# The samples' attention with the cache as the moving operand, and six held splits at the end of a down chain

## The chip, the core and the metric

The kernel runs on one core of a Trainium2 chip. Its engines work side by side, each through its own queue in order: TensorE (PE; its weight loads are PEld) multiplies, VectorE (DVE) and ScalarE (ACT) work elementwise, GpSimd (POOL) does the rest of the elementwise work, and SyncE (SP) issues most of the transfers. Matmul results land in PSUM, of which there are eight banks; the other data is in SBUF, with 128 partitions. The metric is device time in microseconds of one launch.

## The reference

One layer of a decoder trunk is computed for a prompt of 1024 tokens and for 8 samples of one token each. All of it is float32. What bears on the change, cut down:

```python
# attention over a window of 128 keys with sinks; 16 query heads, 4 key heads, head size 64
s = jnp.einsum('...qhgd,...khd->...hgqk', qg, kb) * (SWA_HD ** -0.5)
p = jax.nn.softmax(jnp.concatenate([s, sink], axis=-1), axis=-1)[..., :-1]
return jnp.einsum('...hgqk,...khd->...qhgd', p, vb)
...
# a sample: the cache's last 127 rows and its own new row
kc = jnp.concatenate([st['k'], kk], axis=1)
vc = jnp.concatenate([st['v'], vv], axis=1)
...
x = x + gt2 * ((jax.nn.silu(gc) * up) @ lp['w_ffn_down'])     # 2816 -> 1024
```

Before the attention stand a normalisation and one input projection; beside it runs a gated delta rule with a short convolution; after it an output projection and a feed-forward block with a convolution. The last line is the down projection.

## The kernel before

**Precision.** A large product splits both operands into a high and a low part and adds three matmuls (`mm3`, lines 180 to 182). A split is two instructions: ACT writes the high part (line 129), and VectorE or POOL the rest (line 130). Small products, such as the samples', are plain float32 matmuls. The profile has two matmul records for one of these.

**Order.** The instructions are not queued as the program text has them. A planner simulates the kernel when it is built, and at each moment takes for an engine the ready instruction that is earliest by priority. Priority follows the text, except that `later` and `weave` move pieces back by a number of places, and that `issue_after` forbids instructions to stand ahead of a given one on the same engine. On the chip each queue then runs in the planned order, whatever is ready.

**Attention.** `attention` goes over four groups of query heads, one for each key head, and each group over eight blocks of 128 tokens (`attention_block`). A block's way is: scores on PE (lines 614 and 615), a masked copy (lines 618 and 620), maximum and sink (`m` and `es`, lines 622 to 627), exponentials with their sums (line 630), the inverse denominator `den` (lines 631 and 632), scaling (lines 635 and 637), transposes into `pt` and masks (lines 642 and 646), the value product into `pv` (line 652) and a copy out (line 654). Pieces of other work, such as input projections and convolution tiles (lines 778 to 790), fill the gaps.

**Samples.** `sample_cache` runs before the fourth group. It loads the keys and values of 8 samples into tiles of four samples (`halves`), and lays the queries into `qa`, one block of eight columns for each sample and each pair of key heads; the rest of `qa` is zeroed at line 684 and the copies are at line 688. In the first half of the fourth group, `sample_keys` transposes the keys (line 698), and `sample_softmax` follows: 16 matmuls of 8 columns with a 128 by 128 tile of the cache as the weight (line 708), a copy (line 709) and a transpose to have one query on each partition, the softmax (lines 718 to 727), a transpose back and its copy (line 731), 16 matmuls with the values (line 735), and 16 copies of 64 partitions by 8 columns into `obs` (line 739), which is stored at line 741. All of its PSUM tiles are one bank, one after another.

**The down projection.** `ffn_down` is made of seven products of 11 steps, numbered 5, 3, 4, 7, 1, 2, 6. They stand in chains: 5 and 3, 4 and 7, then 1, 2 and 6. A step is 8 groups of three matmuls, one group for each of eight PSUM banks; product 6 instead finishes one bank after another. At the last step of each of the first six products ACT copies the eight banks out (`take`, line 1784), and a chain starts in these banks anew. VectorE adds these copies to the result (line 1470). The operands of a step come by SP into a raw buffer (lines 1749, 1752 and 1754; five buffers in turn), POOL combines two weights for some products (line 1753), and `part` splits the sum for PE. Steps are counted from 0 to 76 over all products. `fetch_to` keeps the splits 13 steps ahead of PE. In the last steps of a chain it only loads, and the splits come in the text after the chain's copies; `issue_after` then keeps them behind the last copy in ACT's queue.

```python
for ins in (self.last_up, self.last_copy) if 5 <= s < len(tags) else (self.took,) if s >= len(tags) and self.took else ():
...
while done < n if split else begun < n and begun < done + 4 + (begun % 5 != 3):
    if begun == done or not split:
        fetch(begun)
...
fetch_to(s + len(tags), i != c[-1] or g < G - 4)
```

Of the kernel before, what the change touches and what calls it, by code (L numbers as in the profile page):

```python
# [18 lines left out]
P = 128  # L19
NP = 1024  # L20
NS = 8
# [43 lines left out]
class Step:  # L65
# [590 lines left out]
    def sample_cache(self, pool, psum, kx, vx):  # L656
        nc, I = self.nc, self.I

        tp = self.t(self.pmf, [NS, 4, P], "mm")
        for i in range(2):  # L660
            self.transpose(tp[:, i, :], kx[:, i, P:136])
            self.transpose(tp[:, 2 + i, :], vx[:, i, :])
        new = self.t(pool, [NS, 512], "new", bufs=1)
        nc.vector.tensor_copy(new, tp.rearrange("b i c -> b (i c)"))
        newd = self.t(self.dr, [1, 2, NS, 256], "newd")
        for c in range(2):
            nc.sync.dma_start(newd[0, c], new[:, c * 256:(c + 1) * 256])

        kv = []
        for c, (cache, out) in enumerate(((I["cache_swa_k"], self.O[7]), (I["cache_swa_v"], self.O[9]))):  # L670
            halves = []
            for b in (0, 4):
                kc = self.t(pool, [P, 4, 256], "qst")
                nc.sync.dma_start(kc, cache[0][b:b + 4].rearrange("b w g d -> w b (g d)"))
                nc.sync.dma_start(kc[0:1], newd[:, c, b:b + 4])
                halves.append(kc)
            kv.append(halves)
            old = lambda a, w: a[0][:, w:w + 127].rearrange("b w g d -> b (w g d)").rearrange("b (s e) -> s b e", s=16)
            with self.tc.issue_after(self.w_load.ins):
                nc.sync.dma_start(old(out, 0), old(cache, 1))  # L680
            nc.sync.dma_start(out[0][:, 127].rearrange("b g d -> b (g d)"), newd[0, c])

        qa = self.t(pool, [P, 2, NS, 8], "qa", bufs=1)
        nc.gpsimd.memset(qa, 0.0)
        for hq in range(16):
            p, r, g = hq // 8, hq % 8, hq // 4
            src = self.qs[(hq % 2) * 64:(hq % 2) * 64 + 64, hq // 2, :]
            nc.vector.tensor_copy(qa[(g % 2) * 64:(g % 2) * 64 + 64, p, :, r], src)
        self.samples = kv, qa

    def sample_keys(self):
        kc = self.samples[0][0]
        for half in kc:
            for p in range(2):
# [2 lines left out]
                    self.transpose(tp[:, b, :], half[:, b, p * P:(p + 1) * P])  # L697
                self.nc.scalar.copy(half[:, :, p * P:(p + 1) * P], tp)

    def sample_softmax(self, pool, psum):  # L700
        nc, I = self.nc, self.I
        (kc, vc), qa = self.samples

        scores = self.t(pool, [P, 2, NS, 8], "st", bufs=1)
        sc = self.t(self.pmf, [P, 2, NS, 8], "mm")
        for b in range(NS):
            for p in range(2):
                nc.tensor.matmul(sc[:, p, b, :], kc[b // 4][:, b % 4, p * P:(p + 1) * P], qa[:, p, b, :], start=True, stop=True)
        nc.vector.tensor_copy(scores, sc)
        ps = self.t(self.pmf, [P, P], "mm")  # L710
        self.transpose(ps, scores.rearrange("k p b r -> k (p b r)"))

        sk = self.t(pool, [P, 8], "sk", bufs=1)
        sinkc = self.t(pool, [P, 1], "sinkc", bufs=1)
        for p in range(2):
            src = I["swa_sinks"][0][p * 8:p * 8 + 8].rearrange("(r o) -> r o", o=1)
            nc.sync.dma_start(sinkc[p * 64:p * 64 + 64, :], src.unsqueeze(0).broadcast_to([NS, 8, 1]))
        nc.vector.tensor_reduce(sk[:, 0:1], ps, axis=AX.X, op=ALU.max)
        nc.vector.tensor_tensor(sk[:, 0:1], sk[:, 0:1], sinkc, op=ALU.max)
        nc.vector.tensor_tensor(sk[:, 1:2], sinkc, sk[:, 0:1], op=ALU.subtract)  # L720
        nc.scalar.activation(sk[:, 2:3], sk[:, 1:2], AF.Exp)
        nc.vector.tensor_scalar_mul(sk[:, 3:4], sk[:, 0:1], -1.0)
        pr = self.t(pool, [P, P], "pr", bufs=1)
        nc.scalar.activation(pr, ps, AF.Exp, bias=sk[:, 3:4], accum_out=sk[:, 4:5])
        nc.vector.tensor_tensor(sk[:, 5:6], sk[:, 4:5], sk[:, 2:3], op=ALU.add)
        nc.vector.reciprocal(sk[:, 6:7], sk[:, 5:6])
        nc.vector.tensor_scalar_mul(pr, pr, sk[:, 6:7])
        ps = self.t(self.pmf, [P, P], "mm")
        self.transpose(ps, pr)
        pT = self.t(pool, [P, 2, NS, 8], "pT", bufs=1)  # L730
        nc.vector.tensor_copy(pT.rearrange("k p b r -> k (p b r)"), ps)
        pv = self.t(self.pmf, [P, 2, NS, 8], "mm")
        for p in range(2):
            for b in range(NS):
                nc.tensor.matmul(pv[:, p, b, :], vc[b // 4][:, b % 4, p * P:(p + 1) * P], pT[:, p, b, :], start=True, stop=True)
        obs = self.t(pool, [P, 8, NS], "obs", bufs=1)
        for hq in range(16):
            p, r, g = hq // 8, hq % 8, hq // 4
            nc.vector.tensor_copy(obs[(hq % 2) * 64:(hq % 2) * 64 + 64, hq // 2, :],
                                  pv[(g % 2) * 64:(g % 2) * 64 + 64, p, :, r])  # L740
        nc.sync.dma_start(self.ob[:, :, NP:NT].rearrange("i p b -> p i b"), obs)


# [980 lines left out]
    def ffn_down(self, pool, psum):  # L1724

        nc, I = self.nc, self.I
        G, n = FT // 2, NT // 2
        tags = ("bmh2", "bml0", "bml2", "bmh1", "pk2", "bml1", "pk3", "pk6", "pk4", "pk0", "pk5", "pk1", "bmh3")
# [63 lines left out]
        def fetch_to(n, split=True):  # L1792
            nonlocal begun, done
            n = min(n, len(steps))
# [3 lines that stand above are left out]
                    begun += 1  # L1798
                else:
                    part(done)  # L1800
                    done += 1

        for c in chains[:-1]:
            ps = {(p, j): self.t(pl, [P, 512], tag, bufs=k)[:, :256 + 4 * p] for (p, j), (pl, tag, k) in zip(order, banks)}
            for i in c:
                for g in range(G):
                    fetch_to(s + len(tags), i != c[-1] or g < G - 4)
                    for p, j in order:
                        step(s, ps[p, j], p, j, g == 0 and i == c[0], g == G - 1, {"skip_group_check": True} if i != c[0] else {})
                        if g == G - 1:  # L1810
                            take(ps[p, j], i, p, j)
                    if g in range(2, 10):
                        for _ in range(2):
                            if waiting[0] or waiting[1]:
                                add(*(waiting[0] or waiting[1]).pop(0))
                    s += 1
# [253 lines left out]
```

## Time and profile before

| | us |
|---|---|
| median of 3 runs | 2089.26 (2088.08 to 2090.94) |
| the profiled execution | 2091.4 |
| its span | 2089.7 |
| busy: PE, PEld | 2022.6, 1920.9 |
| busy: VectorE, ACT, POOL | 1362.0, 901.3, 515.3 |
| samples' softmax and products, first matmul to the store's issue | 348.66 to 369.06 |
| copies at the ends of the six products | from 1872.94, 1905.62, 1944.16, 1976.16, 2006.93, 2038.47 |

A row of the order in time reads: start, length, engine, line, operation, output<-inputs by the program's names, shapes, count of merged records, and in brackets how long the engine had been idle and what released it. A row of a group has the least, median and longest duration in ns, and the first and last start. Names have their number left out: `mm` is any PSUM tile of that name, `qst` a buffer that holds the cache among others.

### The profile page before, as it was taken

What the parts mean: (1) busy time and instruction counts of PE and PEld (TensorE: products, weight loads), DVE (VectorE), ACT (ScalarE), POOL (GpSimd) and SP (SyncE); (2) the same over time, 40 slices, a digit from 0 to 9 for tenths busy, and PEclk for the clock granted to TensorE, in tenths of its full rate; (3) what the DMA queues carried; (4) which work ended last, traced back from release to release, by engine and by line L of the source; (5) the groups of instructions that cost most, each with busy time, mean ns of one, the idle gap of its engine ahead of it and who ended that gap; (6) DMA issues with size and microseconds to landing.
All of it is one profiled execution on the core that took longest, in us unless ns stands there. A gap on an engine that the chain in (4) does not pass through costs nothing.

```text
span 2089.7 us, 41318 instructions
## 1 busy us (share of the span) xinstructions
PE 2022.6 (97%) x16245; PEld 1920.9 (92%) x16245; DVE 1362.0 (65%) x2734; ACT 901.3 (43%) x2233; POOL 515.3 (25%) x594
## 2 busy tenths in 40 slices
PE   7999999899999999989999999999999999999898
PEld 4987778799999999989988999999999999999898
DVE  4756767573746756556554575478876776768876
ACT  4665544434334343442442452345544544544533
POOL 2000000121321211211111000005566556445521
PEclk9999999999999999999999999999999999999999
DMA  8256443142331322312266774523233233487972
GB/s 291 71 144 209 136 165 115 60 131 58 78 89 53 86 62 59 91 37 60 63 189 194 250 230 122 155 67 97 88 106 113 87 97 102 130 296 262 310 241 86
DMA packets 301887, 275.75 MB, mean 132 GB/s; under 512 B 59730, under 2 KB 248111, under 8 KB 301676
## 3 DMA queue, kind: packets, MB, share of 16 engines
q1 hardware_dynamic: 295642, 252.14, 39.4%
q0 software_dynamic: 5552, 20.37, 2.8%
q8 instruction: 127, 2.08, 0.4%
q14 instruction: 68, 0.56, 0.1%
q10 hardware_dynamic: 498, 0.61, 0.1%
HBM read 212.93 MB, written 62.51 MB: 132 GB/s over the span
## 4 chain that ended last, share of the span: by engine, by line
PE 84%; DMA 6%; DVE 5%; ACT 3%; issue 1%; SPq 1%; POOL 0%; DVEq 0%; POOLq 0%; ACTq 0%
PE mm L180 18%; PE mm L181 18%; PE mm L182 18%; PE wv L180 3%; PE wv L182 3%; PE wv L181 3%; PE wy L182 2%; PE wy L180 2%; PE wy L181 2%; PE pv L652 1%; PE pt L190 1%; DMA raw<-in_w_swa_out_dram 1%; PE tp L190 1%; PE mm L264 1%; PE sc L614 1%
## 5 line engine op out<-in xcount | busy, mean ns | idle before, releaser
L180 PE MATMUL mm<-b1h,wh 128*128 128x384 f32 (+1 forms) x1520 | 498.0, 329 | 2.8 <-ACT gt L1292 1.6
L181 PE MATMUL mm<-b1l,wh 128*128 128x384 f32 (+1 forms) x1520 | 490.2, 323 | 0.0
L182 PE MATMUL mm<-b1h,wl 128*128 128x384 f32 (+1 forms) x1520 | 488.8, 324 | 0.0
L180 PEld LDWEIGHTS mm<-b1h,wh 128*128 128x128 f32 x1520 | 287.2, 189 | 14.4 <-issue 7.1
L182 PEld LDWEIGHTS mm<-b1h,wl 128*128 128x128 f32 x1520 | 286.5, 189 | 5.1 <-issue 4.5
L181 PEld LDWEIGHTS mm<-b1l,wh 128*128 128x128 f32 x1520 | 287.3, 189 | 4.0 <-issue 1.9
L129 ACT ACTIVATE wh<-raw 128x1024 fp32r<-128x1024 f32 x83 | 87.0, 1049 | 126.9 <-PE mm L181 73.7
L130 DVE TENSOR_TENSOR wl<-raw,wh 128x1024 fp32r<-128x1024 f32 x82 | 102.1, 1246 | 55.6 <-ACT wh L129 54.3
L181 PE MATMUL mm<-pk,w 128*128 128x260 f32 (+1 forms) x440 | 124.3, 283 | 1.1 <-DVE pk L130 1.1
L180 PE MATMUL mm<-pk,w 128*128 128x260 f32 (+1 forms) x440 | 124.5, 283 | 0.0
L182 PE MATMUL mm<-pk,w 128*128 128x260 f32 (+1 forms) x440 | 124.1, 282 | 0.0
L130 DVE TENSOR_TENSOR w<-ws,w 128x512 fp32r<-128x512 f32 x88 | 77.9, 887 | 36.6 <-ACT w L129 36.3
L1624 ACT COPY bml<-mm 128x256 f32<-128x256 f32 (+1 forms) x132 | 48.9, 371 | 97.9 <-PE mm L182 94.6
L182 PE MATMUL mm<-bmh,w 128*128 128x260 f32 (+1 forms) x320 | 90.2, 282 | 0.0
L180 PE MATMUL mm<-bmh,w 128*128 128x260 f32 (+1 forms) x320 | 89.9, 281 | 0.0
L1679 DVE SCALAR_TENSOR_TENSOR fa<-fz,fcw,fa 128x512 f32<-128x512 f32 x88 | 75.2, 873 | 18.4 <-ACT fa L1677 18.1
L180 PE MATMUL mm<-b2h,wh 128*128 128x384 f32 (+1 forms) x256 | 83.8, 330 | 2.9 <-ACT wh L129 2.9
L181 PE MATMUL mm<-b2l,wh 128*128 128x384 f32 (+1 forms) x256 | 84.2, 329 | 0.4 <-DVE b2l L130 0.4
L181 PEld LDWEIGHTS mm<-pk,w 128*128 128x128 f32 x440 | 82.8, 188 | 1.3 <-DVE pk L130 1.3
L182 PE MATMUL mm<-b2h,wl 128*128 128x384 f32 (+1 forms) x256 | 83.2, 327 | 0.0
L180 PEld LDWEIGHTS mm<-pk,w 128*128 128x128 f32 x440 | 82.9, 188 | 0.3 <-ACT bml L1624 0.2
L182 PEld LDWEIGHTS mm<-pk,w 128*128 128x128 f32 x440 | 82.9, 189 | 0.0
(649 smaller groups left out, 5914.2 us busy)
## 6 DMA issues: line engine op xcount, KB each, us to landing
raw<-in_w_in_dram SPq DMA_DIRECT2D x59, 512.0 KB
ws<-in_w_ffn_down_dram SPq DMA_DIRECT2D x55, 256.0 KB
raw<-xd SPq DMA_DIRECT2D x47, 258.0 KB
raw<-in_w_ffn_down_dram SPq DMA_DIRECT2D x47, 256.0 KB
raw<-in_w_ffn_gate_dram SPq DMA_DIRECT2D x22, 512.0 KB
raw<-in_w_ffn_up_dram SPq DMA_DIRECT2D x22, 512.0 KB
qst<-in_w_mod_dram SPq DMA_DIRECT2D x16, 512.0 KB
raw<-in_w_mod_dram SPq DMA_DIRECT2D x16, 512.0 KB
```

The source lines that it names most:

```text
L129: self.nc.scalar.activation(hi, x, AF.Copy)
L130: (eng or self.nc.vector).tensor_tensor(lo, x, hi.bitcast(F32), op=ALU.subtract)
L180: mm(ps, whi, xhi, start=first, stop=False, **kw)
L181: mm(ps, whi, xlo, start=False, stop=False, **kw)
L182: self.last_mm = mm(ps, wlo, xhi, start=False, stop=last, **kw).ins
L190: self.nc.tensor.transpose(out, in_, self.ident[:p, :p])
L264: nc.tensor.matmul(ps[32 * j:32 * j + 32], self.cT[:, k0 + j, :], ws[j // 2][:, j % 2, :], start=k0 == 0, stop=k0 > 0)
L614: self.scored = nc.tensor.matmul(sc[:, r, 256 - w:256], q, KH[:, lo:lo + w], start=True, stop=False)
L652: nc.tensor.matmul(pv[64 * r:64 * r + 64], V[:, n - back, ch], ps[:, r::2, :], start=back == 0, stop=back == (n > 0))
L1624: self.last_copy = nc.scalar.copy(r[p, i], x[p])
L1679: nc.vector.scalar_tensor_tensor(ai[:, c:e], zi[:, j + c:j + e], col(j), ai[:, c:e], op0=ALU.mult, op1=ALU.add)
```

## The change

In the samples' attention the cache is now the moving operand. `qa` is wider, 160 columns for each pair of key heads and each half of the samples, and the eight columns of sample i of a half start at column 40 i. A window of 32 columns that starts at 32 i holds them at 8 i, and zeros elsewhere. So four matmuls, one for each sample of a half, add into the same 32 partitions and leave four samples' rows below one another; the four quarters of the partitions are the pairs and halves. The scores arrive with one query on each partition, without a copy and a transpose. After the softmax the transposed probabilities go back into the same places of `qa`, the same 16 matmuls run with the values, and their result is copied and transposed. Queries are laid out by 8 copies of 64 by 16 in place of 16 of 64 by 8, and results by 4 of 64 by 32 in place of 16 of 64 by 8.

In the down projection the splits of the last six steps of a chain are held behind its copies, before it was four.

```diff
-        qa = self.t(pool, [P, 2, NS, 8], "qa", bufs=1)
+        qa = self.t(pool, [P, 2, 2, 160], "qa", bufs=1)
         nc.gpsimd.memset(qa, 0.0)
-        for hq in range(16):
-            p, r, g = hq // 8, hq % 8, hq // 4
-            src = self.qs[(hq % 2) * 64:(hq % 2) * 64 + 64, hq // 2, :]
-            nc.vector.tensor_copy(qa[(g % 2) * 64:(g % 2) * 64 + 64, p, :, r], src)
+        spread = qa.rearrange("k p h (i c) -> k p h i c", c=40)
+        queries = self.qs.rearrange("d (p a q) (h i) -> d p a q h i", p=2, a=2, h=2)
+        for a, c, p in ((a, c, p) for a in range(2) for c in range(2) for p in range(2)):
+            nc.vector.tensor_copy(spread[64 * a:64 * a + 64, p, :, :, 4 * a + c:4 * a + 4:2].rearrange("d h i q -> d q h i"),
+                                  queries[64 * c:64 * c + 64, p, a])
...
+    def sample_product(self, out, wide, halves):
+        for i in range(4):
+            for j in range(4):
+                self.nc.tensor.matmul(out[32 * j:32 * j + 32], wide[:, j // 2, j % 2, 32 * i:32 * i + 32],
+                                      halves[j % 2][:, i, j // 2 * P:(j // 2 + 1) * P], start=i == 0, stop=i == 3)
...
-        scores = self.t(pool, [P, 2, NS, 8], "st", bufs=1)
-        sc = self.t(self.pmf, [P, 2, NS, 8], "mm")
-        for b in range(NS):
-            for p in range(2):
-                nc.tensor.matmul(sc[:, p, b, :], kc[b // 4][:, b % 4, p * P:(p + 1) * P], qa[:, p, b, :], start=True, stop=True)
-        nc.vector.tensor_copy(scores, sc)
         ps = self.t(self.pmf, [P, P], "mm")
-        self.transpose(ps, scores.rearrange("k p b r -> k (p b r)"))
+        self.sample_product(ps, qa, kc)
...
-        pT = self.t(pool, [P, 2, NS, 8], "pT", bufs=1)
-        nc.vector.tensor_copy(pT.rearrange("k p b r -> k (p b r)"), ps)
+        nc.vector.tensor_copy(qa.rearrange("k p h (i c) -> k (p h) i c", c=40)[:, :, :, 0:8],
+                              ps.rearrange("k (j i r) -> k j i r", j=4, i=4))
+        ps = self.t(self.pmf, [P, P], "mm")
+        self.sample_product(ps, qa, vc)
+        nc.vector.tensor_copy(pr, ps)
         pv = self.t(self.pmf, [P, 2, NS, 8], "mm")
-        for p in range(2):
-            for b in range(NS):
-                nc.tensor.matmul(pv[:, p, b, :], vc[b // 4][:, b % 4, p * P:(p + 1) * P], pT[:, p, b, :], start=True, stop=True)
+        self.transpose(pv.rearrange("d p b r -> d (p b r)"), pr)
         obs = self.t(pool, [P, 8, NS], "obs", bufs=1)
-        for hq in range(16):
-            p, r, g = hq // 8, hq % 8, hq // 4
-            nc.vector.tensor_copy(obs[(hq % 2) * 64:(hq % 2) * 64 + 64, hq // 2, :],
-                                  pv[(g % 2) * 64:(g % 2) * 64 + 64, p, :, r])
+        outs = obs.rearrange("d (p a q) b -> d p a q b", p=2, a=2)
+        for a, c in ((a, c) for a in range(2) for c in range(2)):
+            nc.vector.tensor_copy(outs[64 * c:64 * c + 64, :, a],
+                                  pv[64 * a:64 * a + 64, :, :, 4 * a + c:4 * a + 4:2].rearrange("d p b q -> d p q b"))
...
-                    fetch_to(s + len(tags), i != c[-1] or g < G - 4)
+                    fetch_to(s + len(tags), i != c[-1] or g < G - 6)
```

## The prediction

> **What bounds the kernel now.** I read the page first, then stretches of 10 us around the samples' steps, then the order of each engine there and at the joints of the down chains.
>
> ```profile
> PE 2022.6 (97%) x16245; PEld 1920.9 (92%) x16245; DVE 1362.0 (65%) x2734; ACT 901.3 (43%) x2233; POOL 515.3 (25%) x594
> ```
>
> TensorE is busy for 97% of the span. So time is won only where TensorE idles, runs at a low clock, or has work taken away, and none of that is given back while it stays saturated afterwards. The stretches (columns: stretch, length, busy us and instructions of PE, PEld, DVE, ACT, POOL, then granted clock, DMA share, GB/s):
>
> ```profile
> 340.00:370.00 30.00, 25.67 (x177) 22.75 (x175) 21.86 (x69) 14.89 (x52) 1.00 (x1) 0.89 0.20 72
> 370.00:380.00 10.00, 7.36 (x32) 5.70 (x33) 4.30 (x13) 4.88 (x19) 0.51 (x1) 0.74 0.10 24
> 380.00:390.00 10.00, 9.10 (x57) 6.92 (x56) 6.94 (x20) 5.45 (x23) 0.00 (x0) 0.92 0.15 55
> 390.00:400.00 10.00, 10.00 (x72) 9.22 (x71) 5.84 (x17) 6.51 (x23) 1.74 (x2) 1.00 0.12 36
> ```
>
> From 340 to 390 TensorE idles 7.9 us and the clock is down to 0.74; from 390 it is full again. The samples' attention lies at the start of this hole:
>
> ```profile
> 348.66 5.03 PE L708 MATMUL mm<-qa,qst 128*128 128x8 f32 x32 [0.68 <-ACT qst L698]
> 353.54 0.56 PE L614 MATMUL sc<-kh,qst 128*128 128x256 f32 x1
> 354.12 0.41 PE L614 MATMUL sc<-kh,qst 128*128 128x256 f32 x1
> 354.33 0.41 PE L615 MATMUL sc<-kl,qst 128*128 128x256 f32 x1
> 357.53 0.67 PE L190 MATMUL pt<-ident,E 128*128 128x128 f32 x4
> 360.81 0.28 PE L614 MATMUL sc<-kh,qst 128*128 128x256 f32 x1
> 360.93 0.28 PE L615 MATMUL sc<-kl,qst 128*128 128x256 f32 x1
> 362.53 3.64 PE L735 MATMUL mm<-pT,qst 128*128 128x8 f32 x32
> 369.99 0.33 PE L190 MATMUL pt<-ident,E 128*128 128x128 f32 x1 [2.14 <-ACT E L635]
> ```
>
> The two products hold TensorE from 348.66 to 353.54 (4.88 us) and for 3.64 us from 362.53, with 8 columns in each matmul. After the first, scores start 0.21 us apart where 0.12 us is normal: half clock. On VectorE:
>
> ```profile
> 349.61 1.28 DVE L784 SCALAR_TENSOR_TENSOR vch<-raw,cw,vch 128x1024 f32<-128x1024 f32 x1
> 350.81 0.16 DVE L625 TENSOR_TENSOR es<-sink,m 128x4 f32<-128x4 f32 x1
> 353.94 0.15 DVE L631 TENSOR_TENSOR den<-den,es 128x4 f32<-128x4 f32 x1
> 355.20 0.45 DVE L620 COPY_PREDICATED E<-trilu,sc 128x256 f32<-128x256 uint32 x1 [0.89 <-ACT E L618]
> 366.21 2.83 DVE L739 COPY obs<-mm 64x8 f32<-64x8 f32 x16 [1.71 <-PE mm L735]
> 369.06 0.16 DVE L631 TENSOR_TENSOR den<-den,es 128x4 f32<-128x4 f32 x1
> 365.99 0.19 ACT L630 ACTIVATION_READ_ACCUMULATOR E<-E,m 128x1 f32 x1
> ```
>
> The third of the prompt's blocks of this group has its last exponential sum read at 366.18 (365.99 and 0.19), but its den waits to 369.06 behind 16 output copies; the 2.14 us of idle TensorE are this.
>
> **The change part by part.** *Products.* 16 matmuls of 128 columns into 32 output rows replace 16 of 8 columns with 128; both are two records each, 32. The modulation does the new form with 512 columns:
>
> ```profile
> 301.30 0.33 PE L181 MATMUL mm<-b1l,wh 128*128 128x384 f32 x1
> 301.56 0.62 PE L264 MATMUL mm<-wmh,cTr 128*32 128x512 f32 x2
> 302.44 1.04 PE L264 MATMUL mm<-raw,cTr 128*32 128x512 f32 x8
> 303.41 0.45 PE L182 MATMUL mm<-b1h,wl 128*128 128x384 f32 x1
> 303.70 0.33 PE L180 MATMUL mm<-b1h,wh 128*128 128x384 f32 x1
> 303.87 0.34 PE L181 MATMUL mm<-b1l,wh 128*128 128x384 f32 x1
> ```
>
> The records of four output quarters start together, as one round (two and two in the rows at 301.56). Two rounds take 1.04, of which the last record's 0.62 is length, so a round is 0.42 us. With a quarter of the columns I take 0.11, and 8 rounds for 32 records: 0.88. Bounds: 8 rounds of full length, 3.4, above; below, the 0.88 with nothing around it. Going into the narrow form, 301.30 to 301.56 is 0.26 against 0.17 between plain ones (303.70 to 303.87), 0.09 more; coming out, two rounds from 302.44 end at 303.28 and the next starts at 303.41, 0.13. A product is then 1.1 us: the first gives back 3.8 us of TensorE, the second 2.5 (1.4 and 0.2 at the upper bound).
>
> The Trainium skill, "TensorEngine Tiling (Array Packing)", Key Properties, speaks against this: a change of tiling mode drains TensorE. The rows agree, at some 0.1 us a change; without it each product would be 0.9 and the sum 0.4 us lower.
>
> *Around them.* The copy of the scores and their transpose go; a copy and a transpose of the output come. One for one, zero; the new copy is off the prompt's chain. *Output copies*, 16 of 64x8 become 4 of 64x32; *query copies*, 16 become 8 of 64x16:
>
> ```profile
> L739 DVE COPY obs<-mm x16: 157/164/170, 366.2 to 368.9; 64x8 f32<-64x8 f32 x16
> L688 DVE COPY qa<-qs x16: 136/170/173, 96.5 to 297.8; 64x8 f32<-64x8 f32 x16
> 3.66 0.20 POOL L684 MEMSET qa<- 128x128 f32 x1
> 9.56 0.55 POOL L125 TENSOR_TENSOR ss<-ss,mhalf 128x1 f32<-128x1 f32 x1 [2.19 <-DVE ss L288]
> ```
>
> An output copy costs between 0.16 (8 columns) and the 0.45 of the mask copy (256); near the small one, 0.19; four are 0.75, so VectorE is free 2.1 us sooner. The query copies save 8 x 0.17 = 1.4 us of VectorE between 96 and 298, where TensorE does not wait for them: zero. The zeroing of qa grows from 128 to 640 columns, at most five times 0.20, 0.8 more; POOL idles 2.19 us soon after: zero.
>
> *What is late next.* TensorE gets 3.8 + 2.5 us, the 2.1 us wait, and 1.7 us of half clock (the 4.0 us from 353.54 to 357.53 at 0.21 for 0.12): 10.1 us, the most this can give. It won't all arrive, because the prompt's softmax chain then leads. For its first block, es at 350.81 comes behind a convolution step (L784) and does not move, nor does den at 353.94; only the mask copy at 355.20, behind scores queued after the product, goes ahead of den. Scaling and transposes can then follow den at some 355.0 in place of 357.53: 2.6 us. The second block's scores are also early, but it shares ACT and VectorE with the first: I take 1.0 (0 to 3). The third gains the copies' wait, 2.83 us (2.1 to 2.8). Sum 6.4. The clock: I assume that TensorE, waiting from about 352 to 355, falls to half once in either kernel, so nothing is won there. Least: the copies' 2.1 alone.
>
> *Down chains.* From the code: at the end of chains 3, 7, 1 and 2, the splits held until after the chain's copies are now 28-33, 50-55, 61-66, 72-76 (before 30-33, 52-55, 63-66, 74-76). Raw buffers are five, so one load each (33, 55, 66) and its SP and POOL work passes behind the copies too.
>
> ```profile
> 1910.19 1.09 ACT L129 ACTIVATE bml<-bmh 128x1028 fp32r<-128x1028 f32 x1
> 1970.00:1980.00 10.00, 10.00 (x86) 10.00 (x86) 6.17 (x6) 6.35 (x12) 5.70 (x5) 1.00 1.04 382
> 1944.57 0.58 PE L180 MATMUL mm<-pk 128*128 128x256 f32 x1 [6.03 <-ACT bml L1784]
> 1943.20 1.06 ACT L129 ACTIVATE bmh<-bmh 128x1028 fp32r<-128x1028 f32 x1 [2.42 <-POOL bmh L1753]
> 1975.18 1.07 ACT L129 ACTIVATE bmh<-raw 128x1028 fp32r<-128x1028 f32 x1 [0.18 <-POOL raw L1753]
> 2006.93 0.37 ACT L1784 COPY bml<-mm 128x256 f32<-128x256 f32 x1 [7.01 <-PE mm L182]
> 2038.47 0.37 ACT L1784 COPY bml<-mm 128x256 f32<-128x256 f32 x1 [4.37 <-PE mm L182]
> 2047.10 1.21 DVE L130 TENSOR_TENSOR pk<-bmh,pk 128x1028 fp32r<-128x1028 f32 x1
> 2047.90 0.60 PE L190 MATMUL wy<-ident,x 128*128 128x128 f32 x4
> ```
>
> At the end of 3, split 28 runs at 1910.19, behind the copies already: zero. The large wait, 6.03 us, is at the joint from 4 to 7, in mid-chain, where splits are not held before or after: it stays. At the end of 7, one split runs to 1976.25 just ahead of the copies, but TensorE is busy for all of 1970 to 1980: zero. At the end of 1 and of 2, ACT had been idle 7.01 and 4.37 us when the copies came: no gain. Cost: before the last chain (2), VectorE's halves of the held splits begin at 2047.10 behind the gated adds. Five in place of three end 2 x 1.21 = 2.4 us later. The copies of 2 begin at 2038.47, one per output group of three matmuls (0.36 us at 0.12 each); the first group ended at about 2038.1, so the other seven last to some 2040.7. From there TensorE has three output groups of six ready steps (3 x 6 x 0.36 = 6.5 us) and 19 transposes (16 of normed rows, 3 of convolution rows) of 0.11 (2.1 us), to 2049.3; the halves come from 2048.3 on, every 1.2 us: nearly covered. I take 0.5, from 0 to 2.4; without the interleaving of three groups it would be 7.
>
> Sum: the profiled execution took 2091.4 (span 2089.7 and 1.7 around it); 2091.4 - 6.4 + 0.5 = 2085.5. It ran 2.1 above the median, 2089.26; on the median's scale 2083.4.
>
> **The rivals.** *The gain drowns* in the softmax chain: blocks 1 and 2 are paced by ACT and VectorE, and TensorE only waits longer. For: VectorE is over 70% busy from 340 to 370. Against: its worst wait is for samples' work. It gives 1 to 2.5 us: 2087.5.
>
> *The clock stays up.* If the new wait of about 3 us doesn't bring half clock, the half clock behind the 2.14 us row goes too (the 0.74 in 370 to 380): 1.5 us more, half of some 3 us, 2081.9. Against: that row itself, where 2.14 us and the thin product before it were enough.
> The Trainium skill, "TensorE: Matmul & The Clock Gate", Part 1, lets the clock fall only after an idle window of some 3.4 us, which would make this case the likelier.
>
> *The wait at 1938 closes.* It exists since splits that POOL fed late sit ahead of the copies in ACT's queue. If the planner, with loads passing later, lays two fewer there, 6.0 go: 2077.4. Against: those splits are not among the held ones.
>
> *Slower: more splits ahead of the copies at the mid-chain joints*, where nothing holds them (5 to 3, 4 to 7). A split costs up to 1.06 plus its 2.42 wait for POOL, 3.5 us. The later loads push POOL's work toward these joints. Three more cost 10.5: 2083.4 + 10.5 = 2093.9; from three on this decides the sign. For: the 6.03 us shows that the planner misjudges such a joint. Against: the other mid-chain joint has no wait.
>
> *The last chain runs dry*: 7 in place of 0.5, 2089.9.
>
> **How the numbers follow.** Forecast 2083.4 (its own range 2080 to 2087) 0.35; drowned gain 0.17; the clock up 0.10; closed wait 0.12; more splits 0.16; dry last chain 0.10. A measurement tells about 0.2%, 4.2 us, from no change: faster is under 2085.1, slower over 2093.4. Faster: 0.30 of the forecast's, 0.10 clock, 0.12 closed wait, 0.01 of the drowned: 0.53. Slower: 0.15 of the more-splits case, 0.04 of the dry chain and 0.01: 0.20. The rest, 0.27. The range, 2077 to 2094, leaves half of the closed-wait and of the more-splits case outside.
>
> **What would show it.** Right: products of about 1.1 us, four records starting together; the den after them not behind 16 copies; the third block's transposes about 6 us sooner; 6.03 us still at the joint 4 to 7; no ACT split within 2 us ahead of the copies of 7, 1 and 2. Wrong: rounds near 0.43 us, or plain matmuls between them; TensorE's full busy share again only from 390; another wait before a copy in the down chains; idle TensorE from 2043 to 2055.

## The result and the profile after

The changed kernel takes 2087.56 us (median of 14 runs, 2085.91 to 2092.80) against 2091.55 us of the kernel before in the same comparison (14 runs, 2087.29 to 2096.51). The ratio is 0.9981, 95% interval [0.9971, 0.9991]: 4 us won, with 2 to 6 inside the interval. The forecast, 2083.4 beside a median of 2089.26, was a gain of 5.9 us, a ratio of 0.9972, just inside the interval.

The profiled execution of after took 2086.13 us (span 2084.4), 5.3 less than that of before. The page's first part, and then the same stretches as in the prediction (columns as there), from the trace of after:

```profile
PE 2012.7 (97%) x16245; PEld 1910.2 (92%) x16245; DVE 1347.8 (65%) x2714; ACT 900.2 (43%) x2233; POOL 520.2 (25%) x594
```

```profile
340.00:370.00 30.00, 23.23 (x209) 17.96 (x207) 23.94 (x71) 19.31 (x69) 1.52 (x2) 1.00 0.22 74
370.00:380.00 10.00, 7.63 (x49) 5.44 (x49) 5.96 (x21) 6.09 (x27) 0.00 (x0) 1.00 0.14 55
380.00:390.00 10.00, 10.00 (x71) 8.73 (x70) 6.42 (x17) 5.55 (x19) 1.69 (x2) 1.00 0.13 39
2045.00:2050.00 5.00, 3.41 (x22) 2.53 (x21) 4.92 (x22) 1.80 (x5) 1.12 (x2) 0.88 0.30 116
2050.00:2055.00 5.00, 5.00 (x35) 4.96 (x34) 3.35 (x12) 0.96 (x4) 1.10 (x2) 0.78 0.51 202
```

In the samples' part the granted clock was 1.00 throughout, where before had 0.89, 0.74 and 0.92, and TensorE is full again from 380. New is what the last two rows show: within the last chain TensorE stands for 1.6 us and then runs at a low clock. The samples' steps, and two waits, in the order of time on TensorE:

```profile
347.41 1.08 PE L704 MATMUL mm<-qst,qa 128*32 128x128 f32 x32 [0.68 <-ACT qst L699]
353.39 0.38 PE L614 MATMUL sc<-kh,qst 128*128 128x256 f32 x1 [2.35 <-DVE E L620]
355.02 0.60 PE L190 MATMUL pt<-ident,E 128*128 128x128 f32 x4
356.99 1.08 PE L704 MATMUL mm<-qst,qa 128*32 128x128 f32 x32
363.36 0.60 PE L190 MATMUL pt<-ident,E 128*128 128x128 f32 x4
1933.72 0.58 PE L180 MATMUL mm<-pk 128*128 128x256 f32 x1 [5.56 <-ACT bml L1786]
2046.70 0.63 PE L190 MATMUL wv<-ident,x 128*128 128x128 f32 x4 [0.99 <-DVE x L1477]
2048.56 0.84 PE L190 MATMUL wv<-ident,x 128*128 128x128 f32 x4 [0.49 <-DVE raw L1896]
```

Both products take 1.08 us. The wait at the joint from 4 to 7 is still there (5.56 for 6.03). At 2046.70 and 2048.56 TensorE waits for VectorE, which it did not before.

Three stretches of TensorE's time hold the whole difference, worked out from the starts of the same matmuls in both traces. *Samples' stretch*: from the 305th to the 1217th matmul of 128x384 with a full 128x128 weight (137.4 to 504.6 before), 367.2 us before and 358.9 after, 8.3 less. *Middle*: from there to the first matmul of the last chain, 1536.1 and 1536.4. *Last chain*: from that matmul to TensorE's last start, 41.0 and 45.6, 4.6 more. The head, up to the 305th, was 1.9 us shorter (135.5 for 137.4). That is scatter of single executions: e2 below, which leaves the samples' part as before, has 134.9 there, and before has three windows of half clock in its first 30 us where after and e2 have one. -1.9 - 8.3 + 0.3 + 4.6 is the -5.3 of the two profiled executions. So the samples' part gave more than forecast and the down chains' part took most of the difference back. Over all runs below the middle goes from 1532.0 to 1540.4 us, so single executions are compared by stretches only, and what a change is worth is taken from the medians.

### The profile page after: what moved, and what is told of

Read it like the earlier page. It is cut to its first block, busy times and chain, and to the rows that moved or that the text cites. A ratio compares the mean times of both kernels' runs of the same rounds, so it can differ in the third digit from the quotient of the medians.

```text
span 2084.4 us, 41297 instructions
## 1 busy us (share of the span) xinstructions
PE 2012.7 (97%) x16245; PEld 1910.2 (92%) x16245; DVE 1347.8 (65%) x2714; ACT 900.2 (43%) x2233; POOL 520.2 (25%) x594
## 4 chain that ended last, share of the span: by engine, by line
PE 83%; DVE 5%; DMA 5%; ACT 3%; issue 1%; SPq 1%; POOL 1%; DVEq 0%; POOLq 0%; ACTq 0%
PE mm L180 19%; PE mm L181 18%; PE mm L182 18%; PE wv L180 3%; PE wv L182 3%; PE wv L181 3%; PE wy L182 2%; PE wy L180 2%; PE wy L181 2%; PE pv L652 1%; PE pt L190 1%; PE tp L190 1%; DVE x L1472 1%; PE mm L264 1%; PE rc L954 1%
```

## The experiments

In the table, the ratio is that of the medians to the kernel before in the same comparison, with its 95% interval; the stretches are those defined above, each from one profiled execution and good to 0.1 us; the windows are the stretches of 3.41 us at half clock between 340 and 400 us, of which more below.

| run | ratio | samples' stretch | windows | last chain |
|---|---|---|---|---|
| before | 1 | 367.2 | 4 | 41.0 |
| after | 0.9981 [0.9971, 0.9991] | 358.9 | 0 | 45.6 |
| e1, samples' part alone | 0.9959 [0.9946, 0.9971] | 360.0 | 1 | 41.2 |
| e2, six held, alone | 1.0029 [1.0016, 1.0043] | 367.3 | 5 | 45.6 |
| e3, four at the end of 2, six elsewhere | 0.9972 [0.9962, 0.9983] | 360.0 | 1 | 45.0 |
| e4, four at all joints | 0.9957 [0.9943, 0.9971] | 360.5 | 1 | 41.2 |
| e5, copies alone | 0.9997 [0.9986, 1.0008] | 366.0 | 5 | 41.2 |
| e6, products alone | 0.9970 [0.9960, 0.9981] | 361.6 | 2 | 41.0 |
| e7, first product alone | 0.9980 [0.9968, 0.9993] | 362.4 | 2 | 41.2 |
| e8, second product alone | 0.9980 [0.9971, 0.9990] | 362.3 | 2 | 40.9 |
| e9, six at the end of 2 alone | 0.9973 [0.9956, 0.9989] | 359.8 | 1 | 42.8 |
| e10, six at the end of 1 alone | 0.9985 [0.9970, 1.0000] | 362.2 | 2 | 45.2 |
| e11, three combines left out | 0.9970 [0.9956, 0.9984] | 360.1 | 1 | 41.9 |
| e12, eight at the joint 4 to 7 | 0.9981 [0.9966, 0.9996] | 359.0 | 0 | 41.0 |

**The two halves of the change.** The samples' part alone, on the changed kernel:

```diff
-                    fetch_to(s + len(tags), i != c[-1] or g < G - 6)
+                    fetch_to(s + len(tags), i != c[-1] or g < G - 4)
```

> The samples' part of the change alone, with splits held over the last four steps as before. Theory (the samples' part gives about 8 us, the down chains lose about 5 of it again before the last chain): 8 us under the kernel before, ratio 0.996; from 2040 to 2055 of the span TensorE stays full at a granted clock of 1.00, and the granted clock between 340 and 390 is 1.00. Rival (the held splits cost nothing, and what the trace of after shows at 2045 is an accident of that execution): as the whole change, 4 us, 0.998.

And the reverse edit on the kernel before, `G - 4` to `G - 6`:

> The down chains' part alone, on the kernel before. Theory: slower by 4 to 5 us, ratio 1.002, all of it before the last chain: TensorE idle for some 1.6 us between 2050 and 2060 of the span, behind VectorE's halves of five splits, and a granted clock under 0.9 in the two stretches of 5 us after it; nothing at the ends of chains 3, 7 and 1; the wait of 6 us at the joint from 4 to 7 is still there. Rival: the same time as before, ratio 1.000.

Both times came out as the theory had them. The samples' part is worth 8.6 us (0.9959 of 2091.23), the held splits cost 6 us (0.0029 of it, 3 to 9 inside the interval); the last chains of 41.2 and 45.6 us say where. Two details did not. In e1 the granted clock was not 1.00 throughout from 340 to 390: one window of half clock stands there. And in e2 the low clock stood in one stretch of 5 us, not in two: after and e2 have one window of 3.41 us at half clock in the last chain, which in after lies across two stretches.

**Inside the samples' part.** Only the copies: both products stay 16 matmuls of 8 columns, and the copies go in groups.

```diff
+        queries = self.qs.rearrange("d (p a q) b -> d p a q b", p=2, a=2)
+        for a, c, p in ((a, c, p) for a in range(2) for c in range(2) for p in range(2)):
+            nc.vector.tensor_copy(qa[64 * a:64 * a + 64, p, :, 4 * a + c:4 * a + 4:2].rearrange("d b q -> d q b"),
+                                  queries[64 * c:64 * c + 64, p, a])
...
+        for a, c in ((a, c) for a in range(2) for c in range(2)):
+            nc.vector.tensor_copy(outs[64 * c:64 * c + 64, :, a],
+                                  pv[64 * a:64 * a + 64, :, :, 4 * a + c:4 * a + 4:2].rearrange("d p b q -> d p q b"))
```

> The kernel before with only the copies in groups of four (8 query copies, 4 output copies); both products stay 16 matmuls of 8 columns. Theory (the samples' part gives 8 us: about 2 to 3 by the copies through the third block, the rest by the products and by a clock that doesn't fall): 2.5 us under before, 0.9988; half clock after the first product still there (granted clock 0.9 in 340 to 370). Rival (the copies' wait of 2.14 us was what let the clock fall in 370 to 380, and its going carries the gain): 4 to 5 us, 0.998.

The rival falls. The theory's 0.9988 is just inside the interval of 0.9997 [0.9986, 1.0008], and so is no gain at all; the stretch is 366.0 us against 367.3 with as many windows, five, in e2. On VectorE the copies are what was priced (four in 0.80 us, first row), but the products beside them stay, and the clock falls there. Then TensorE's two products and, in the last two rows, the stretches at half clock:

```profile
369.05 0.80 DVE L739 COPY obs<-mm 64x32 f32<-64x32 f32 x4 [2.26 <-PE mm L735]
```

```profile
347.35 5.91 PE L708 MATMUL mm<-qa,qst 128*128 128x8 f32 x32 [0.68 <-ACT qst L698]
363.73 5.28 PE L735 MATMUL mm<-pT,qst 128*128 128x8 f32 x32
```

```profile
348.57:358.81 10.24, 10.24 (x46) 9.49 (x45) 6.28 (x21) 5.68 (x24) 0.00 (x0) 0.50 0.13 53
365.64:372.47 6.83, 6.83 (x31) 6.73 (x31) 3.20 (x13) 1.75 (x7) 0.00 (x0) 0.50 0.07 5
```

Half clock begins 1.2 and 1.9 us into a product of 8-column matmuls, while the records show TensorE busy for all of the time (10.24 of 10.24, 6.83 of 6.83).

The opposite, new products with the 16 output copies of before:

```diff
-        outs = obs.rearrange("d (p a q) b -> d p a q b", p=2, a=2)
-        for a, c in ((a, c) for a in range(2) for c in range(2)):
...
+        for hq in range(16):
+            p, r, g = hq // 8, hq % 8, hq // 4
+            nc.vector.tensor_copy(obs[(hq % 2) * 64:(hq % 2) * 64 + 64, hq // 2, :],
+                                  pv[(g % 2) * 64:(g % 2) * 64 + 64, p, :, r])
```

> The samples' part with the products as changed, but the output copied in 16 pieces of 64 by 8 as before; splits as before. Theory: 5.5 us under before, ratio 0.9974; granted clock 1.00 from 340 to 365; the third block's den waits behind the 16 copies again for some 2.1 us, and TensorE behind it. Rival (the den is no longer behind the copies, since the product ends earlier than its sums): 8 us, 0.996.

6.3 us of the 8.6 come without the grouped output copies, near the theory's 5.5. The rival's 0.996 is the end of the interval; by the trace it falls: a den does wait behind the 16 copies again, TensorE stood 2.83 us up to 362.72, and a window of half clock followed at 363.9, a little ahead of where the theory let the clock stay full; rows of VectorE:

```profile
359.09 2.81 DVE L741 COPY obs<-mm 64x8 f32<-64x8 f32 x16
361.94 0.16 DVE L631 TENSOR_TENSOR den<-den,es 128x4 f32<-128x4 f32 x1
```

What the grouping adds on top is not settled: the intervals of e1 and e6 overlap, and the stretch with 16 copies and two windows, 361.6, is no longer than the one with four copies and two windows, 362.2 in e10.

Then one product at a time. With the second in the old form, on the probabilities as transposed:

```diff
-        self.sample_product(ps, qa, vc)
...
+                nc.tensor.matmul(pv[:, p, b, :], vc[b // 4][:, b % 4, p * P:(p + 1) * P], pT[:, p, b, :], start=True, stop=True)
```

> The samples' part, but only the first product (scores) in the new form; the second is 16 matmuls of 8 columns on the 128 probabilities. Theory (the clock falls in or just after a run of 8-column matmuls, and a wait of 2.4 us with full matmuls around it doesn't lower it): clock 1.00 until the second product, then half clock for some us right after that product; 5 us under before, 0.9976. Rival (it is the idle time of more than 2 us that lowers the clock, in both products alike): no half clock after either product as long as no wait of 3 us stands there, 6 us, 0.997.

And with the first in the old form:

```diff
-        self.sample_product(ps, qa, kc)
...
+                nc.tensor.matmul(sc[:, p, b, :], kc[b // 4][:, b % 4, p * P:(p + 1) * P],
+                                 qa[:, p, b // 4, P + 8 * (b % 4):P + 8 * (b % 4) + 8], start=True, stop=True)
```

> The samples' part, but only the second product (output) in the new form; the scores are 16 matmuls of 8 columns and are copied and transposed as before. Theory: half clock right after the first product, for about 4 us, as before, none after the second; 4 us under before, 0.998. Rival (half clock after the first product costs nothing, since the prompt's softmax chain leads there): 6 us, 0.997.

Each alone gives 4 us (0.9980), 4.8 and 4.9 of the stretch; by their times theory and rival of e7 can't be told apart, by the clock they can. The clock falls with whichever product is left in 8 columns: its row, and the stretch at half clock, first of e7, then of e8.

```profile
358.96 4.96 PE L736 MATMUL mm<-pr,qst 128*128 128x8 f32 x32
```

```profile
361.23:368.06 6.83, 6.81 (x32) 5.42 (x32) 3.29 (x11) 2.33 (x10) 0.00 (x0) 0.50 0.07 5
```

```profile
346.85 5.27 PE L715 MATMUL mm<-qa,qst 128*128 128x8 f32 x32 [0.68 <-ACT qst L699]
```

```profile
348.77:355.60 6.83, 6.83 (x31) 6.73 (x31) 4.41 (x15) 3.75 (x14) 0.00 (x0) 0.50 0.20 79
```

So the new form pays twice: by its shorter products, and by the windows of half clock that came with a product in 8 columns in each of these four rows. The rival of e7, that idle time alone lowers the clock, falls: no wait of 3 us stands there. How product and idle time count together is worked out next.

**What a wait of 2.35 us does to the clock.** It stands in after and in e1 alike. In after no window fell to half clock; in e1 one did, at the end of that wait, and the matmul behind it took 0.58 for 0.38 (its row, then the window ahead of the fall and the fallen one):

```profile
353.14 0.58 PE L614 MATMUL sc<-kh,qst 128*128 128x256 f32 x1 [2.35 <-DVE E L620]
```

```profile
349.42:352.83 3.41, 1.26 (x8) 0.74 (x6) 3.23 (x16) 3.34 (x15) 0.00 (x0) 1.00 0.00 0
352.83:356.24 3.41, 3.10 (x11) 3.00 (x12) 1.31 (x7) 2.64 (x14) 0.00 (x0) 0.50 0.37 154
```

Of the eight executions with the whole samples' part, two had no window of half clock, five had one and one had two. The stretch goes with it: 358.9 and 359.0 with none, 359.8 to 360.5 with one, 362.2 with two.

In before, the windows lie at these places:

```profile
350.84:357.67 6.83, 6.83 (x30) 6.73 (x31) 4.45 (x19) 4.11 (x16) 0.00 (x0) 0.50 0.20 79
371.32:374.73 3.41, 3.41 (x12) 2.90 (x14) 2.72 (x7) 0.64 (x2) 0.00 (x0) 0.50 0.00 0
378.15:381.56 3.41, 3.09 (x11) 2.99 (x12) 1.95 (x7) 1.08 (x3) 0.00 (x0) 0.50 0.01 2
```

Their starts, 350.84, 371.32 and 378.15, are 6 and 2 times 3.41 apart: the clock changes on a grid of such windows. In each of the fourteen executions all starts of half clock lie on one such grid, and it lies differently on the code each time. The Trainium skill, "TensorE: Matmul & The Clock Gate", Part 1, says that the window is free-running and lasts 3413 ns; the trace agrees, with 3.41 us.

Whether a wait of 2.35 us costs a window depends on how it falls on the grid. In e1 a line of the grid, at 352.83, stands near the end of the wait: the window before it has 2.15 us of idle TensorE (3.41 less 1.26), and the next is at half clock. In after the line is at 352.41 and cuts the wait in two:

```profile
349.00:352.41 3.41, 1.94 (x12) 1.42 (x10) 3.38 (x12) 3.05 (x12) 0.00 (x0) 1.00 0.00 0
352.41:355.82 3.41, 2.34 (x15) 2.05 (x15) 2.00 (x12) 3.31 (x18) 0.00 (x0) 1.00 0.37 154
```

With 1.47 and 1.07 us idle neither is followed by half clock. It is the same in all eight: at most 1.39 and 1.47 us of the wait in one window in the two executions where the clock stayed up, 1.88 to 2.35 us in the six where it fell.

The products in 8 columns fit the same count if their time is added to the idle time. From 60 to 2060 us the fourteen executions have 8074 windows of the grid at full clock. Half clock follows each of the 87 windows that have 1.83 us or more of the two together, none of the 7948 with less than 1.46, and 15 of the 39 between. The plainest case of a product is in e2, where the second one begins at 359.86: TensorE is busy for the whole window (first row), and half clock follows (second row).

```profile
358.85:362.26 3.41, 3.41 (x32) 3.37 (x30) 2.73 (x7) 0.71 (x5) 0.00 (x0) 1.00 0.00 0
362.26:372.50 10.24, 9.40 (x38) 7.16 (x37) 6.31 (x26) 2.86 (x12) 0.00 (x0) 0.50 0.05 3
```

**Where the held splits cost.** First the end of 2 back to four, the ends of 3, 7 and 1 at six:

```diff
-                    fetch_to(s + len(tags), i != c[-1] or g < G - 6)
+                    fetch_to(s + len(tags), i != c[-1] or g < G - (4 if i == 2 else 6))
```

> The whole change, but the end of the last chain of this kind (product 2) holds the splits of four steps, as before, and the ends of 3, 7 and 1 hold six. Theory (only the end of 2 costs anything): as the samples' part alone, 8 us under the kernel before, 0.996. Rival (the loads that pass behind the copies at the other ends cost as well, spread out): between, 4 to 6 us under before, 0.9975.

The theory fell. The last chain takes 45.0 us although only three splits are held before it, and the gain is 0.9972. So the cost was put there by an earlier chain. VectorE and GpSimd at the end of 2, with the samples' part alone (on VectorE a stretched add, two adds of the usual length and the first half of a held split; then GpSimd's combines):

```profile
2033.51 1.52 DVE L1472 SCALAR_TENSOR_TENSOR x<-bml,mT,x 128x252 f32<-128x252 f32 x1
2035.03 0.47 DVE L1472 SCALAR_TENSOR_TENSOR x<-bml,less,x 128x252 f32<-128x252 f32 x1
2037.87 0.15 DVE L1477 TENSOR_TENSOR x<-x,gtmp 128x8 f32<-128x8 f32 x1
2040.91 1.21 DVE L130 TENSOR_TENSOR pk<-bmh,pk 128x1028 fp32r<-128x1028 f32 x1
```

```profile
2031.31 1.28 POOL L1755 TENSOR_TENSOR raw<-raw,ws 128x512 f32<-128x512 f32 x1 [2.71 <-DMA ws<-in_w_ffn_down_dram]
2033.27 1.48 POOL L1755 TENSOR_TENSOR raw<-raw,ws 128x512 f32<-128x512 f32 x1 [0.68 <-DMA ws<-in_w_ffn_down_dram]
```

And in after:

```profile
2030.62 1.52 DVE L1472 SCALAR_TENSOR_TENSOR x<-bml,mT,x 128x256 f32<-128x256 f32 x1
2034.12 1.25 DVE L1477 TENSOR_TENSOR x<-x,gtmp 128x8 f32<-128x8 f32 x1
2038.17 0.72 DVE L1477 TENSOR_TENSOR x<-x,gtmp 128x8 f32<-128x8 f32 x1
2038.82 1.23 DVE L130 TENSOR_TENSOR pk<-raw,pk 128x1028 fp32r<-128x1028 f32 x1
```

```profile
2030.42 1.43 POOL L1755 TENSOR_TENSOR bmh<-bmh,ws 128x512 f32<-128x512 f32 x1 [1.37 <-DMA ws<-in_w_ffn_down_dram]
2033.87 1.47 POOL L1755 TENSOR_TENSOR raw<-raw,ws 128x512 f32<-128x512 f32 x1 [2.02 <-DMA ws<-in_w_ffn_down_dram]
2035.86 3.01 POOL L1755 TENSOR_TENSOR raw<-raw,ws 128x512 f32<-128x512 f32 x1 [0.52 <-DMA ws<-in_w_ffn_down_dram]
```

An add of 0.47 us takes 1.52 when a combine of GpSimd runs, and one of 8 columns takes 1.25 in place of 0.15: the latter ends when the combine ends (2035.37 and 2035.34). In after three adds lose 2.7 us so, in e1 one loses 1.05; with two more halves of 1.2 us behind them, VectorE is through with the halves 13.8 us after the last chain begins, where e1 needs 9.9. The Trainium skill, "SBUF — State Buffer", Who interferes with whom, states the rule: a VectorE instruction with two SBUF inputs and a GpSimd instruction that reads SBUF take turns, each for its whole length. The adds that stretch have both inputs in SBUF, so the trace agrees.

A new theory: GpSimd's combines fall on the adds since the load of step 66 is held behind the copies of 1. Two runs with six at one place alone, first the end of 2, then the end of 1 (`6 if i == 2 else 4` and `6 if i == 1 else 4` in the line above):

> The samples' part, and six steps' splits held at the end of 2 alone, four at the ends of 3, 7 and 1. From the last chain's first matmul to TensorE's last start took 41.2 us with the samples' part alone, 45.6 with the whole change, 45.0 with six at 3, 7 and 1 and four at 2. Theory (the loss comes from the load of step 66, which passes behind the copies of 1 with GpSimd's combines behind it, so that they later fall on VectorE's gated adds): 41.2 to 42, no more than one add of over 1 us among the adds of 2. Rival (the two further halves of 1.2 us each cost by themselves): 43.5 or more.

> The samples' part, and six steps' splits held at the end of 1 alone, four at 3, 7 and 2. Theory (as for the run with six at 2 alone: the late load of step 66 carries the loss): the last chain takes about 45.0 us, as with six at 3, 7 and 1, and three adds of 2 take over 1 us, each ending with a combine of GpSimd; about 4 us over the samples' part alone. Rival (the ends of 3 and 7 push GpSimd's work late): 41.2.

Six at the end of 1 alone gives a last chain of 45.2 us, as the theory had it: three adds of over 1 us, and TensorE idle behind them.

```profile
2032.23 1.56 DVE L1472 SCALAR_TENSOR_TENSOR x<-bml,less,x 128x256 f32<-128x256 f32 x1
2034.97 1.50 DVE L1472 SCALAR_TENSOR_TENSOR x<-bml,less,x 128x256 f32<-128x256 f32 x1
2036.79 1.26 DVE L1476 TENSOR_TENSOR gtmp<-bml,mT 128x8 f32<-128x8 f32 x1
```

```profile
2042.34 0.67 PE L190 MATMUL wv<-ident,x 128*128 128x128 f32 x4 [2.48 <-DVE x L1477]
```

The adds explain half of this. They lose 3.2 us, 2.2 more than in e1, but VectorE begins the first half of a held split 4.1 us later in the last chain than in e1 (10.5 us for 6.3). The other 2 us are that the adds start late, at 2031.83, 0.1 us behind the start of the last chain where e1 is 1.9 ahead of it. The late combines reach ScalarE too: a split that waits for GpSimd stands ahead of the copies of 2.

```profile
2029.58 1.07 ACT L129 ACTIVATE pk<-bmh 128x1028 fp32r<-128x1028 f32 x1 [1.17 <-POOL bmh L1755]
2030.56 0.35 ACT L1786 COPY bml<-mm 128x256 f32<-128x256 f32 x1
```

In e3 it is the same (first add at the start of the last chain); in after and e9 the copies come in time.

GpSimd's combines of steps 66 and 67, one row each of e10 and of e1 (last chains from 2031.7 and 2034.6), begin 22 us ahead of the last chain with six held at 1, and 35 us ahead with four:

```profile
2009.63 3.62 POOL L1755 TENSOR_TENSOR raw<-raw,ws 128x512 f32<-128x512 f32 x2 [37.67 <-DMA raw<-xd]
```

```profile
1999.63 2.53 POOL L1755 TENSOR_TENSOR raw<-raw,ws 128x512 f32<-128x512 f32 x2 [24.50 <-DMA raw<-xd]
```

Six at the end of 2 alone gives 42.8, 1.6 over e1 and between the theory's 42 and the rival's 43.5: the two further halves have a price too, a smaller one.

Last, the combines themselves, taken off the adds:

```diff
-            if len(src) > 1:
+            if len(src) > 1 and s < 74:
```

> The whole change, but the last three steps of product 6 (74 to 76) use the first of their two weight blocks alone: the second block isn't loaded and GpSimd doesn't combine, so that the output isn't the reference's. It takes GpSimd's combines off the adds of 2 and leaves the five halves of 1.2 us behind these adds. Theory (the combines hold VectorE up, 2.7 us in three adds where the samples' part alone has 1.05): no add of 2 over 1 us, the last chain takes 43 us or less, against 45.6. Rival (the five halves are the cost): still 45 or more.

41.9 us, with no add over 1 us: 3.7 of the 4.4 us over e1 go with three combines of GpSimd and the loads of their second blocks, while all five halves remain. The theory holds. Together e9 and e11 put 0.7 to 1.6 us to the halves and the rest to the combines, but the two do not simply add. What decides is how late VectorE is through with the halves: 9.9 us after the last chain begins in e1, 11.1 in e11, 11.9 in e9, and 13.8 to 14.0 in e3, after, e2 and e10. Only these four have a window of half clock in the last chain, and only they take 45 us or more.

**The wait at the joint from 4 to 7.** Four steps held at every joint, then eight at this one:

```diff
+                    fetch_to(s + len(tags), g < G - 4)
...
+                    fetch_to(s + len(tags), i == 5 or g < G - (8 if i == 4 else 4))
```

> The samples' part, and splits held over the last four steps of every chain, at the joints inside a chain (5 to 3, 4 to 7) too. Theory (the 6 us at the joint from 4 to 7 are waits for splits that stand ahead of the copies in ScalarE's queue): the wait goes, 5 to 6 us more than the samples' part alone, 13.5 us under before, 0.9935. Rival one: the next steps' splits are late instead, TensorE waits for them within some 8 us of the joint, no more than the samples' part alone, 0.996. Rival two: the joint 5 to 3, which had no wait, gets one, 0.998.

> The samples' part, four steps' splits held at the ends of 3, 7, 1 and 2, and eight at the joint from 4 to 7, so that the splits of steps 37 to 44 come behind the copies of 4 on ScalarE. With four held there, ScalarE still had the split of step 39 ahead of the copies, 2.4 us behind GpSimd's combine of it. Theory: the wait of 5 to 6 us at this joint goes, as TensorE has 13 to 19 us of lead on those splits: 5 us under the samples' part alone, 13 under before, ratio 0.9935. Rival (the loads that pass behind the copies make GpSimd late for chains 7 and 1, as at the end): the wait goes, but it comes back in 7 or 1, ratio 0.996 or more.

With four the wait stays (5.86 us) and the time is that of e1, so the theory of e4 falls. With eight no wait is left there, but at the next joint, from 7 to 1, a larger one stands, behind three splits that each wait for GpSimd ahead of the copies of 7 (the row of TensorE, then the last split and the first copy on ScalarE):

```profile
1966.59 0.58 PE L180 MATMUL mm<-bml 128*128 128x256 f32 x1 [7.79 <-ACT bml L1786]
```

```profile
1965.22 1.06 ACT L129 ACTIVATE bmh<-raw 128x1028 fp32r<-128x1028 f32 x1 [1.14 <-POOL raw L1755]
1966.19 0.35 ACT L1786 COPY bml<-mm 128x256 f32<-128x256 f32 x1
```

The rival holds: what GpSimd does not do ahead of one joint it does ahead of the next. 0.9981 is 4.6 us more than e1's 0.9959, with intervals that just overlap; 2.8 of it would be this wait's 7.79 against e1's 5.0, and the rest is not explained, as the profiled execution, 2081.62, was among the fastest of its run. The best versions tried are e1 and e4, 0.9959 and 0.9957, better than both kernels (their intervals end where that of after begins) and not told apart from one another.

## Why the prediction was right, and where its sum was not

*Products, 1.1 us each*: right, 1.08, four records starting together every 0.11 us, and no plain matmul between them.

*Output copies, 2.1 us of VectorE*: right as a length (0.80 for 2.83). That all of it would reach TensorE, as "Least: the copies' 2.1 alone" has it, was not shown: copies alone gave a ratio of 0.9997, with both 2.1 us and nothing inside the interval.

*The softmax chain leads*: right in kind. The first block's transposes stand at 355.02, where some 355.0 was forecast; as the product had begun 1.25 us sooner, the block gained 1.3, not 2.6. The wait for the mask copy is there, with 2.35 us for the 3 assumed. The third block's transposes came at 363.36 for 369.99, 6.6 us sooner (forecast: about 6), 5.4 of it from this part.

*"I assume that TensorE, waiting from about 352 to 355, falls to half once in either kernel, so nothing is won there"*: this is the step that failed in the samples' part. Half clock in before was four windows of 3.41 us, two at the thin product and two behind the wait of 2.14 us; the changed kernel has none, one or two. The stretch gave 8.3 us for the 6.4 of the sum, 7.2 with one window. In this execution the rival "the clock stays up" came true, and its further 1.5 us is near the 1.9 that the sum lacked. Which of the two comes is decided by how the wait falls on the grid of windows, and neither had that; the idle window of some 3.4 us that the prediction names behind this rival was not needed, as 1.83 us of one window were always enough.

*Ends of 3, 7 and 1 at zero*: right for TensorE's time at these ends: TensorE has no wait there, no split of ScalarE stands within 2 us ahead of the copies of 7, 1 and 2, and the middle stretch is as before (1536.1, 1536.4). What failed is the end of 1: "one load each (33, 55, 66) and its SP and POOL work passes behind the copies too" was written down and given no price. It is most of the price: the load of step 66 makes GpSimd's combines 13 us late, onto the adds of 2 and, in e3 and e10, ahead of the copies of 2 as well.

*The last chain, "0.5, from 0 to 2.4"*: the bounded term that failed, 4.6 measured. The halves were weighed (2.4 us, nearly covered; 1.6 in e9, 0.7 of it left when the combines go), the adds were taken at their length without GpSimd, and the small adds and norm rows that stand behind the halves on VectorE, for which TensorE's transposes wait, were not counted. The rival of a dry last chain, 7, named the place but not the cause, and of the signs for being wrong, idle TensorE from 2043 to 2055 came true.

*The wait at 1938*: right that it stays; holding splits did not remove it either, as e4 left it and e12 moved it to the next joint. The rivals of a closed wait and of more splits ahead of the copies at a mid-chain joint did not come about in after; e12 brought about a wait like the latter's at the end of 7.

So the forecast was near the result with two wrong terms of opposite sign: 1.9 us too little won, 4.1 us too little lost. That the whole came out within 2 us of the forecast is in part luck.

## What to carry to other kernels

Give every transfer and every combine that a reordering passes behind something a price of its own on each queue, and look for it a whole chain later, not only at the joint where it is moved. Where VectorE's work on two SBUF operands bounds a stretch, lay GpSimd's work elsewhere: here each combine of 1.4 to 3.0 us added 0.6 to 1.1 us to an add. Add up TensorE's short waits by windows of 3.41 us, not one by one. And make matmuls of few columns wide if the operands allow it: their cost here was also the half clock that came with them.

## What the runs showed of the hardware

Matmuls of 8 columns can come with a fall of the clock although the records show TensorE without a gap (e5: granted clock 0.50 over 10.24 us, busy 10.24). In seven of the eight such products of before, e2, e5, e7 and e8 it fell within the product and stayed down for two or three windows. The second of before ran at full clock: a line of the grid, at 364.50, cut it into 1.80 and 1.67 us, and the clock fell 5 us behind it, after a wait.

Half clock comes in multiples of 3.41 us on a grid that lies differently in each execution. A window with 1.83 us or more of idle time and 8-column matmuls was always followed by half clock (87 of 87), one with less than 1.46 never. So the same code had none, one or two windows; one was worth about 1.1 us of the samples' stretch, and the two of e10 3.3.

An add of 8 columns on VectorE took 1.25 us for 0.15 beside one GpSimd combine, and the combine suffers as well: 3.01 us, for 1.28 where it meets no add, when it runs into several.
